# A pad of 96 bytes in front of nine weight buffers, and nine different starts inside them

## The chip, the cores and the metric

The kernel runs on one core of one Trainium2 chip. The metric is device time in microseconds (us) of one execution, the median of several. A profile of one execution stands beside it; its engines are called PE (TensorE, matmuls), PEld (TensorE's weight loads), DVE (VectorE), ACT (ScalarE), POOL (GpSimd) and SP (the queue that issues nearly all transfers).

## What is computed

A trunk of two layers over 256 tokens of width 2048, in float32. Each layer is an attention (two kinds side by side in layer 0, a differential one in layer 1), a cross-attention to 256 memory tokens and an MLP, each between two norms:

```
h = h + rms_norm(attention(rms_norm(h)) @ w_out)
h = h + rms_norm(memory_cross_attention(rms_norm(h), mem_n, wq, wk, wv, wo))
u = relu(rms_norm(h) @ w_up)          # 2048 -> 8192
h = h + rms_norm((u * u) @ w_down)    # 8192 -> 2048
```

Nearly all of the time is spent in products of 256 tokens with weights that are read once.

## The kernel before

**Three matmuls for a product.** Every float32 operand is kept as two parts, a rounded one and the rest (`[:, 0]` and `[:, 1]` of a tile). `mm3` (L252) makes a product of three matmuls: high by high, high by low, low by high. A matmul has a *stationary* operand (128 x 128, brought in by a weight load) and a *moving* one (up to 512 columns that stream through). Each of the matmuls here has a weight load of its own, which runs on PEld while the matmul before it streams.

**Weights.** `Weights.load` (L174) brings 256 rows x 512 columns (512 KB) into `raw`; ACT writes the rounded part into a tile `w` (L185 or, with a gain, L190), DVE the rest (L186, L191). `w` comes from the pool `wp` with `NW = 9` buffers in rotation, called homes here. At most nine are alive (`live`), so ACT's next split waits until PE has used up a home. Eleven of the `w` tiles in the whole program lie elsewhere ("spare", in tiles of attention that are free at the time).

**Three shapes of work on PE.** `in_step` (L259): stationary a slice of `xT` (the activations), moving a row of 512 columns of `w`; 6 matmuls for a home and a token tile. `out_block` (L287): stationary a slice of `lt`, moving `w`; a chunk is 12 matmuls, 6 from one home and 6 from the next, then the same two homes for the other token tile. `up` (L683), for 15 of 16 groups of each layer's MLP: the other way round, stationary a slice of `w`, moving `xT`; for each of 64 places in a block a matmul of 512 columns (L715) and one of 256 (L716). An `up` block is followed by an `out_block` of 96 matmuls that uses the `ut` of the group before.

**Behind an `up` block** its four sums lie in three PSUM banks `at` and in one of the three banks `mm`. `split_u` (L671) takes them in two pairs: ACT copies one half of a bank to `ue` (L676), DVE adds the other half to it (L677), then ACT does relu and square (L678, L679) and both engines split the result. The next `out_block` takes the other two `mm` banks for its first two chunks and this one for its third.

**Order.** PE's instructions stand in the order in which the code issues them (a `Line` of delayed calls mixes the attention pieces in). The order on ACT and DVE is made by the scheduler from what each buffer allows.

**Where things lie.** The pools lay tiles one behind the other in each partition's memory. In the built program `xT` begins at byte 33,920, the first home at 71,200 and the others every 8,192 bytes, `lt` at 207,904 (or at 187,424 where `qT`'s buffer is used), `qT` at 187,424, `kT` at 169,504, `v` at 177,696. Every slice that a matmul reads begins at a multiple of 512 bytes inside its tile. So a home's rows begin a multiple of 512 bytes from those of `lt`, and 96 bytes short of a multiple of 512 from those of `xT`. `kT`, `qT` and `v` are whole multiples of 512 from one another too.

Of the kernel before, what the change touches and what calls it, by code (L numbers as in the profile page):

```python
# [11 lines left out]
F32 = mybir.dt.float32  # L12
F32R = mybir.dt.float32r
# [5 lines left out]
P = 128  # L19
D = 2048  # L20
S = 256
# [7 lines left out]
NA_KW = 16  # L29
NW = 9  # L30
NPB = 2
NG = 16
D_TR, D_EV, D_ROPE = 8, 3, 8
SW_GAP, SW_T, SW_M = 4, 8, 7
# [36 lines left out]
def trunk(  # L71
# [6 lines left out]
    V, A, G, PE = nc.vector, nc.scalar, nc.gpsimd, nc.tensor  # L78

    keep = ctx.enter_context(tc.tile_pool(name="keep", bufs=1))  # L80
    wp = ctx.enter_context(tc.tile_pool(name="wp", bufs=NW))
    rawp = ctx.enter_context(tc.tile_pool(name="rawp", bufs=3))
    gp = ctx.enter_context(tc.tile_pool(name="gp", bufs=1))
    sb = ctx.enter_context(tc.tile_pool(name="sb", bufs=1))
# [35 lines left out]
    class Line:  # L120
        def __init__(self):
            self.now, self.q, self.n = 0, [], 0
# [29 lines left out]
    class Weights:  # L152
        def __init__(self):
            self.specs, self.tiles, self.n, self.wait, self.open = [], {}, 0, [], set()
            self.goal, self.live = -1, 0

        def plan_in(self, src, n0, g, spare=(), gate=None):

# [7 lines left out]
        def plan_out(self, src, k0):  # L166
# [4 lines left out]
                    self.specs.append((src, k0 + 2 * kp, n * 512, None, None, None))  # L171
            return a

        def load(self, j):  # L174
            src, k0, n0, tag, _, g = self.specs[j]
            raw = rawp.tile([P, 2, 512], F32, tag="raw", name="raw")
            nc.sync.dma_start(
                raw, src[k0 * P : (k0 + 2) * P, n0 : n0 + 512].rearrange("(k p) n -> p k n", p=P)
            )
            if tag is None:  # L180
                w = wp.tile([P, 2, 2, 512], F32R, tag="w", name="w")
            else:
                w = sb.tile([P, 2, 2, 512], F32R, tag=tag, bufs=1, name="w")
            if g is None:
                A.copy(w[:, 0], raw)  # L185
                V.tensor_tensor(w[:, 1], raw, w[:, 0].bitcast(F32), ALU.subtract)  # L186
            else:
                for kk in range(2):
                    gk = gains[:, g * KT + k0 + kk : g * KT + k0 + kk + 1]
                    A.activation(w[:, 0, kk], raw[:, kk], AF.Copy, scale=gk)  # L190
                    V.scalar_tensor_tensor(  # L191
                        w[:, 1, kk], raw[:, kk], gk, w[:, 0, kk].bitcast(F32), ALU.mult, ALU.subtract
                    )
            self.tiles[j] = w
# [74 lines left out]
    def in_block(u, evac, lag=0, between=None):  # L269

        pts = {}
        for i in range(8 + lag):
            for t, kp in enumerate((i, i - lag)):
                if not 0 <= kp < 8:
                    continue
                if kp == 0:
                    pts[t] = mm_ps()
                in_step(pts[t], u, kp, t)
                if kp == 7 and lag:
                    evac(t, pts[t])  # L280
                    if between is not None:
                        between(t)
        if not lag:
            for t in range(NT):
                evac(t, pts[t])
# [69 lines left out]
    class Leave:  # L355
# [10 lines left out]
        def __call__(self, t, n, c):  # L366
# [3 lines left out]
            if n == 3 and c.space != bass.MemoryType.PSUM:  # L370
                ys[3] = sb.tile([P, 512], F32, tag="p", bufs=NPB, name="y3")
            V.tensor_tensor(ys[n], c, self.post[:, n * 512 : (n + 1) * 512], ALU.mult)
# [76 lines left out]
    def qT_tile():  # L449
        return sb.tile([P, 2, NT, 4, P], F32R, tag="qT", bufs=1, name="qT")  # L450
# [16 lines left out]
    def softmax(sc, bias=None, snk=None):  # L467

        p = sb.tile([P, NT, S], F32, tag="p", bufs=NPB, name="p")
        m = sm.tile([P, NT], F32, tag="m", name="m")  # L470
# [117 lines left out]
    def plan_rest(l, o):  # L588
# [5 lines left out]
        U["up", l, 0] = W.plan_in(mlp_w_up[l], 0, G_MLP + l, ("qT", "kT", "v"), ("up", l))  # L594
        for g in range(NG):
            if g + 1 < NG:
                U["up", l, g + 1] = W.plan_in(mlp_w_up[l], 512 * (g + 1), G_MLP + l)
# [38 lines left out]
    def mem_x(t, n):  # L636
        d = sb.tile([P, 4, P], F32, tag="mt", bufs=2, name="mt")
        nc.sync.dma_start(d, memT[:, t, 4 * n : 4 * n + 4, :])
        split_x(t, n, d)
        I.x[t, n] = "mem"  # L640
# [10 lines left out]
    def mem_and_mlp(l, R, kT, nxt):  # L651
        qT = qT_tile()

        def between(t):
            for n in range(4):
                mem_x(t, n)

        in_block(U["mq", l], evac_T(qT, R, q=True, ev=D_EVM), lag=L_MQ, between=between)
        v = v_tile()
        hd = Heads(qT, kT, lambda i: i, v, lambda i: i, tags=("pT", "pT", "qT", "kT"), lag=(ME_GAP, ME_T, ME_M)).start(M_AT, mix=False)  # L660
        in_block(U["mv", l], evac_V(v, RSM), lag=L_MV)
        for i in range(4):
            line.until(lambda: hd.pT[i] is not None)
            hd.mix(i)
        lv = Leave(gain(mem_post_g[l : l + 1]), G_MLP + l)
        hd.finish()
        W.free(("up", l))
        out_block(U["mo", l], hd.lt, True, lv, stagger=True)
        R = lv.next

        def split_u(ut, j, pts):  # L671

            s = sb.tile([P, 512], F32, tag="p", bufs=NPB, name="s")
            for i, pt in enumerate(pts):
                e = sb.tile([P, S], F32, tag="ue", bufs=2, name="ue")
                A.copy(e, pt[:, S:])  # L676
                V.tensor_tensor(s[:, i * S : (i + 1) * S], pt[:, :S], e, ALU.add)  # L677
            A.activation(s, s, AF.Relu)  # L678
            A.activation(s, s, AF.Square)  # L679
            d = [ut[:, a, j : j + 2, :].rearrange("p k c -> p (k c)") for a in range(2)]  # L680
            split_to(d[0], d[1], s)

        def up(g):  # L683
            ut = lt_tile(("lt", "qT")[g % 2])
            if g == 0:
                left = [0, 1]

                def ev(t, pt):
                    q = sb.tile([P, 512], F32, tag="q", bufs=2, name="u")
                    A.activation(q, pt, AF.Relu)  # L690

                    def turn():
                        tp = tr_ps()
                        for i in range(4):
                            PE.transpose(tp[:, i * P : (i + 1) * P], q[:, i * P : (i + 1) * P], ident)
                        s = sb.tile([P, 512], F32, tag="p", bufs=NPB, name="s")
                        A.activation(s, tp, AF.Square)
                        sv = s.rearrange("p (k c) -> p k c", c=P)
                        split_to(ut[:, 0, :, t * P : (t + 1) * P], ut[:, 1, :, t * P : (t + 1) * P], sv)

                    line.later(D_EVU, turn)

                in_block(U["up", l, 0], ev, lag=L_UP)
                return ut
            pts = [at_ps() for _ in range(3)] + [mm_ps()]
            for kp in range(8):
                w = W.get(U["up", l, g] + kp)
                for t in range(NT):
                    line.until(lambda: I.has_x(t, kp // 2, False))
                for nt in range(4):  # L710
                    for kk in range(2):
                        kt = 2 * kp + kk
                        wn = [w[:, a, kk, nt * P : (nt + 1) * P] for a in range(2)]
                        both = xT[:, kt].rearrange("p a t c -> p (a t c)")
                        PE.matmul(pts[nt], wn[0], both, start=kt == 0, stop=False)  # L715
                        PE.matmul(pts[nt][:, :S], wn[1], both[:, :S], start=False, stop=kt == KT - 1)  # L716
                    if nt == 3:
                        W.done(U["up", l, g] + kp)
                    line.tick()
            for b in range(2):  # L720
                split_u(ut, 2 * b, pts[2 * b : 2 * b + 2])
            return ut

        uts = {0: up(0)}
        lv = None
        for g in range(NG):
            if g + 1 < NG:
                uts[g + 1] = up(g + 1)
            last = g == NG - 1
            if last and l == 0:  # L730
                W.free("odd")
            if last:
                eps = []
                for r in R:
                    q = sm.tile([P, 1], F32, tag="r2", name="r2")
                    V.tensor_tensor(q, r, r, ALU.mult)
                    V.reciprocal(q, q)
                    V.tensor_scalar(q, q, q, NEPS, ALU.mult, ALU.mult)
                    eps.append(q)
                lv = Leave(gain(mlp_post_g[l : l + 1]), nxt, eps)  # L740
            out_block(U["dn", l, g], uts.pop(g), g == 0, lv, stagger=last)
        return lv.next
# [41 lines left out]
    for c in START[2]:  # L784
        t = int(c.lower() == "b")
# [190 lines left out]
```

## Time and profile before

| | us |
|---|---|
| median of 3 runs | 2392.57 (2389.25 to 2392.69) |
| the profiled execution's own time | 2397.27 |
| its span, first to last instruction | 2395.4 |
| PE busy | 2368.5 (99%) |
| DVE busy | 1611.1 (67%) |
| ACT busy | 1373.6 (57%) |

The own time is 1.87 us more than the span. A row of the timeline that ends in xN stands for N instructions of one kind in a row; its second number runs from the start of the first to the end of the last. A matmul's own duration (some 390 ns at 512 columns) is longer than its distance to the next one, since they are pipelined: the distance is (length of the row - duration of one) / (N - 1).

### The profile page before, as it was taken

How to read it: one execution, taken by the hardware profiler on the slowest of the kernel's cores; microseconds unless marked ns; L12 is line 12 of the kernel's file. 1: busy time of each engine (PE TensorE's matmuls, PEld its weight loads, DVE VectorE, ACT ScalarE, POOL GpSimd, SP SyncE). 2: the span in 40 equal slices, each digit the busy share in tenths (PEclk: the TensorE clock that was granted, in tenths of full speed). 3: DMA queues.
4: the chain of work that ended last, by engine and by line, in shares of the span. 5: the costliest groups of instructions: out<-in, count | busy, mean ns of one | idle time of the engine just before them, and what ended most of it. 6: DMA issues, size and time to landing. Idle time of an engine off the chain costs nothing.

```text
span 2395.4 us, 32033 instructions
## 1 busy us (share of the span) xinstructions
PE 2368.5 (99%) x11687; PEld 1984.7 (83%) x11687; DVE 1611.1 (67%) x2545; ACT 1373.6 (57%) x2280; POOL 27.6 (1%) x46
## 2 busy tenths in 40 slices
PE   8999999999999999999999999999999999999998
PEld 6788887888888888888888888887888888888887
DVE  5775678856666656656875666787665666666666
ACT  6756567765555545545665645676754555555553
POOL 0000000000000000000000000000000000000000
PEclk9999999999999999999999999999999999999999
DMA  7657665565665666665555555555656566666663
GB/s 240 214 173 236 185 200 181 180 201 186 192 195 183 194 194 181 196 195 186 184 188 169 168 183 170 197 176 174 201 193 193 184 197 191 187 194 185 192 195 114
DMA packets 238278, 451.88 MB, mean 189 GB/s; under 512 B 21288, under 2 KB 22184, under 8 KB 237352
## 3 DMA queue, kind: packets, MB, share of 16 engines
q1 hardware_dynamic: 237832, 449.32, 59.1%
q8 instruction: 91, 1.49, 0.3%
q14 instruction: 67, 0.55, 0.1%
q10 hardware_dynamic: 288, 0.52, 0.1%
HBM read 445.59 MB, written 5.15 MB: 188 GB/s over the span
## 4 chain that ended last, share of the span: by engine, by line
PE 92%; DMA 3%; DVE 3%; ACT 1%; issue 1%; POOL 0%; SPq 0%; DVEq 0%; POOLq 0%; ACTq 0%
PE mm L254 60%; PE at L715 14%; PE at L716 7%; PE mm L715 5%; PE mm L716 2%; PE at L254 2%; DVE w L191 1%; DMA raw<-in_even_w_in 1%; DMA raw<-in_mem_wv 1%; DMA raw<-in_mem_wo 1%; DMA mt<-memT 1%; PE tr L432 1%; PE tr L345 1%; PE at L502 1%; DMA h<-in_x 0%
## 5 line engine op out<-in xcount | busy, mean ns | idle before, releaser
L254 PE MATMUL mm<-w,lt 128*128 128x512 f32 x4032 | 928.1, 390 | 0.0
L254 PEld LDWEIGHTS mm<-w,lt 128*128 128x128 f32 x4032 | 752.6, 188 | 156.3 <-DVE lt L396 0.3
L191 DVE SCALAR_TENSOR_TENSOR w<-raw,gains,w 128x512 fp32r<-128x512 f32 x944 | 678.1, 746 | 271.4 <-ACT w L190 269.8
L190 ACT ACTIVATE w<-raw,gains 128x512 fp32r<-128x512 f32 x944 | 636.1, 717 | 362.6 <-PE mm L254 269.4
L254 PE MATMUL mm<-w,xT 128*128 128x512 f32 x2784 | 689.6, 401 | 1.2 <-ACT q L424 0.8
L186 DVE TENSOR_TENSOR w<-raw,w 128x1024 fp32r<-128x1024 f32 x336 | 411.1, 1224 | 386.6 <-ACT w L185 386.1
L254 PEld LDWEIGHTS mm<-w,xT 128*128 128x128 f32 x2784 | 515.9, 190 | 115.7 <-ACT q L424 1.2
L185 ACT CAST w<-raw 128x1024 fp32r<-128x1024 f32 x336 | 352.1, 1048 | 448.9 <-PE mm L716 337.2
L715 PE MATMUL at<-xT,w 128*128 128x512 f32 x1440 | 514.8, 393 | 0.0
L716 PE MATMUL at<-xT,w 128*128 128x256 f32 x1440 | 401.8, 279 | 0.0
L715 PEld LDWEIGHTS at<-xT,w 128*128 128x128 f32 x1440 | 269.8, 187 | 64.2
L716 PEld LDWEIGHTS at<-xT,w 128*128 128x128 f32 x1440 | 270.0, 187 | 1.2
L309 DVE TENSOR_TENSOR y<-mm,y 128x512 f32<-128x512 f32 x256 | 175.3, 685 | 16.1 <-PE mm L254 15.9
L715 PE MATMUL mm<-xT,w 128*128 128x512 f32 x480 | 178.3, 393 | 0.0
L716 PE MATMUL mm<-xT,w 128*128 128x256 f32 x480 | 133.9, 279 | 0.0
L715 PEld LDWEIGHTS mm<-xT,w 128*128 128x128 f32 x480 | 89.9, 187 | 21.5
L716 PEld LDWEIGHTS mm<-xT,w 128*128 128x128 f32 x480 | 89.9, 187 | 0.0
L676 ACT COPY ue<-at 128x256 f32<-128x256 f32 x90 | 33.4, 371 | 31.1 <-PE mm L715 28.6
L396 DVE TENSOR_TENSOR lt<-s,lt 128x512 fp32r<-128x512 f32 x64 | 44.0, 688 | 3.6 <-ACT lt L395 3.6
L254 PEld LDWEIGHTS at<-kT,qT 128*128 128x128 f32 x240 | 35.7, 196 | 11.8 <-ACT qT L395 5.3
L254 PE MATMUL at<-kT,qT 128*128 128x256 f32 x240 | 38.5, 294 | 6.8 <-ACT qT L395 4.4
L318 ACT ACTIVATE junk<-y 128x512 bf16<-128x512 f32 x32 | 20.1, 629 | 38.9 <-DVE y L304 38.8
(113 smaller groups left out, 1063.0 us busy)
## 6 DMA issues: line engine op xcount, KB each, us to landing
raw<-in_mlp_w_up SPq DMA_DIRECT2D x256, 512.0 KB, 3.8
raw<-in_mlp_w_down SPq DMA_DIRECT2D x256, 512.0 KB, 4.2
raw<-in_odd_w_in SPq DMA_DIRECT2D x96, 512.0 KB, 4.3
raw<-in_even_w_in SPq DMA_DIRECT2D x72, 512.0 KB, 4.6
raw<-in_even_w_out SPq DMA_DIRECT2D x32, 512.0 KB, 4.4
raw<-in_odd_w_out SPq DMA_DIRECT2D x32, 512.0 KB, 3.8
mt<-memT SPq DMA_DIRECT2D x32, 256.0 KB, 4.2
raw<-in_mem_wk SPq DMA_DIRECT2D x16, 512.0 KB, 4.2
```

What stands on the lines that cost most here:

```text
L185: A.copy(w[:, 0], raw)
L186: V.tensor_tensor(w[:, 1], raw, w[:, 0].bitcast(F32), ALU.subtract)
L190: A.activation(w[:, 0, kk], raw[:, kk], AF.Copy, scale=gk)
L191: V.scalar_tensor_tensor(w[:, 1, kk], raw[:, kk], gk, w[:, 0, kk].bitcast(F32), ALU.mult, ALU.subtract)
L254: PE.matmul(pt, lhs(a), rhs(b), start=first and i == 0, stop=last and i == 2)
L309: V.tensor_tensor(ysl, pt, ysl, ALU.add)
L345: PE.transpose(pt[:, i * P : (i + 1) * P], h[:, t, k * P : (k + 1) * P], ident)
L396: V.tensor_tensor(lo, src, hi.bitcast(F32), ALU.subtract)
L432: PE.transpose(tp[:, i * P : (i + 1) * P], u[:, i * P : (i + 1) * P], ident)
L676: A.copy(e, pt[:, S:])
L715: PE.matmul(pts[nt], wn[0], both, start=kt == 0, stop=False)
L716: PE.matmul(pts[nt][:, :S], wn[1], both[:, :S], start=False, stop=kt == KT - 1)
```

## The change

A tile of 24 float32 numbers (96 bytes) is put in front of the pool `wp`. The rotation of nine buffers becomes nine tiles `wa` to `wi` of one buffer each, taken in turn, each 64 numbers (256 bytes) longer than a home needs; a home begins `HOMES[i]` numbers into its tile, that is 0, 4, 8, 12, 16, 24, 240, 248 and 48 bytes. `ue` has one buffer in place of two.

```diff
+X_SHIFT = 24
+HOMES = (0, 1, 2, 3, 4, 6, 60, 62, 12)
...
-    wp = ctx.enter_context(tc.tile_pool(name="wp", bufs=NW))
+    shift = ctx.enter_context(tc.tile_pool(name="shift", bufs=1))
+    shift.tile([P, X_SHIFT], F32, name="shift")
+    wp = ctx.enter_context(tc.tile_pool(name="wp", bufs=1))
...
-            self.goal, self.live = -1, 0
+            self.goal, self.live, self.turn = -1, 0, -1
...
+        def home(self):
+
+            i = self.turn = (self.turn + 1) % NW
+            c, e = "abcdefghi"[i], HOMES[i]
+            t = wp.tile([P, 2 * 2 * 512 + 64], F32R, tag=f"w{c}", name=f"w{c}")
+            return t[:, e : e + 2 * 2 * 512].rearrange("p (a k n) -> p a k n", a=2, k=2)
...
-                w = wp.tile([P, 2, 2, 512], F32R, tag="w", name="w")
+                w = self.home()
...
-                e = sb.tile([P, S], F32, tag="ue", bufs=2, name="ue")
+                e = sb.tile([P, S], F32, tag="ue", bufs=1, name="ue")
```

In the built program the tiles `wa` to `wi` now begin at 71,296 and every 8,448 bytes (33 x 256), and what lies behind them moves too: `lt` to 210,304 (or 189,824), `qT` to 189,824, `kT` to 171,904, `v` to 180,096. `xT` stays. Taken modulo 256, `xT`, `lt`, `qT`, `kT`, `v` and the tiles `wa` to `wi` all begin at 128, so that a home's distance from both `xT` and `lt` is its own offset (modulo 512 every second home is 256 away from `xT`, and the others from `lt`).

PE's and SP's instructions stand in the same order as before. On ACT and DVE the order changes behind each `up` block. ACT's rows of one block, before (`ue<-at` and `ue<-mm` are the copies of `split_u`, `s<-s` relu and square, `lt<-s` the split's first half, `w<-raw` the splits of weights):

```order
L676 COPY ue<-at 128x256 x3
L190 ACTIVATE w<-raw,gains 128x512
L678 ACTIVATE s<-s 128x512
L676 COPY ue<-mm 128x256
L679 ACTIVATE s<-s 128x512
L190 ACTIVATE w<-raw,gains 128x512
L395 CAST lt<-s 128x512
```

and of the change (its lines are 11 further down):

```order
L687 COPY ue<-at 128x256 x2
L201 ACTIVATE we<-raw,gains 128x512
L689 ACTIVATE s<-s 128x512
L687 COPY ue<-at 128x256
L690 ACTIVATE s<-s 128x512
L201 ACTIVATE we<-raw,gains 128x512
L406 CAST lt<-s 128x512
L687 COPY ue<-mm 128x256
```

The copy from the bank `mm` moves from the fourth copy in a row of six instructions to a place behind the first pair's relu, square and split. DVE's rows of the same block, before (`s<-mm` is the addition that is the last to read the bank `mm`, `y<-mm` takes the sum of a chunk of the next `out_block`):

```order
L677 TENSOR_TENSOR s<-at,ue 128x256 x3
L191 SCALAR_TENSOR_TENSOR w<-raw,gains,w 128x512
L677 TENSOR_TENSOR s<-mm,ue 128x256
L309 TENSOR_TENSOR y<-mm,y 128x512
L396 TENSOR_TENSOR lt<-s,lt 128x512
```

and of the change:

```order
L688 TENSOR_TENSOR s<-at,ue 128x256 x2
L202 SCALAR_TENSOR_TENSOR we<-raw,gains,we 128x512
L688 TENSOR_TENSOR s<-at,ue 128x256
L320 TENSOR_TENSOR y<-mm,y 128x512
L407 TENSOR_TENSOR lt<-s,lt 128x512
L688 TENSOR_TENSOR s<-mm,ue 128x256
```

The last read of the bank `mm` moves behind the first chunk's `y<-mm` and the first pair's `lt<-s`.

## Rows read from the trace of the kernel before

**Rows 1.** The page: span, busy time by engine, granted clock of TensorE by slices.

```profile
span 2395.4 us, 32033 instructions
...
PE 2368.5 (99%) x11687; PEld 1984.7 (83%) x11687; DVE 1611.1 (67%) x2545; ACT 1373.6 (57%) x2280; POOL 27.6 (1%) x46
...
PEclk9999999999999999999999999999999999999999
```

**Rows 2.** Groups by line and shape, PE: busy us, mean ns, idle before.

```profile
L254 PE MATMUL mm<-w,lt 128*128 128x512 f32 x4032 | 928.1, 390 | 0.0
...
L254 PE MATMUL mm<-w,xT 128*128 128x512 f32 x2784 | 689.6, 401 | 1.2 <-ACT q L424 0.8 <-DVE v L400 0.5
...
L715 PE MATMUL at<-xT,w 128*128 128x512 f32 x1440 | 514.8, 393 | 0.0
...
L715 PE MATMUL mm<-xT,w 128*128 128x512 f32 x480 | 178.3, 393 | 0.0
```

**Rows 3.** Waits, longest first: who waited for whom, us in total, times, longest.

```profile
ACT w L185 <- PE mm L716: 337.2, 194, 1.8
...
ACT w L190 <- PE mm L254: 269.4, 160, 3.2
...
PE at L572 <- DMA graw<-in_mem_norm_g: 6.0, 1, 6.0
PE at L254 <- ACT qT L395: 4.4, 3, 2.1
```

**Rows 4.** Timeline of PE: an up block and the out_block behind it.

```profile
1013.60 0.40 PE L715 MATMUL at<-xT,w 128*128 128x512 f32 x1
...
1035.89 0.28 PE L716 MATMUL mm<-xT,w 128*128 128x256 f32 x1
1036.01 21.96 PE L254 MATMUL mm<-w,lt 128*128 128x512 f32 x96
```

**Rows 5.** Timeline of PE: a long row of in_steps, and attention matmuls of 256 columns.

```profile
1329.76 14.21 PE L254 MATMUL mm<-w,xT 128*128 128x512 f32 x60
1343.81 0.87 PE L254 MATMUL at<-kT,qT 128*128 128x256 f32 x6
```

**Rows 6.** Timeline of PE in narrow windows behind a change of form.

```profile
1036.01 2.01 PE L254 MATMUL mm<-w,lt 128*128 128x512 f32 x8
...
1037.40 2.21 PE L254 MATMUL mm<-w,lt 128*128 128x512 f32 x9
...
1294.40 2.00 PE L254 MATMUL mm<-w,lt 128*128 128x512 f32 x8
...
1317.11 2.03 PE L254 MATMUL mm<-w,xT 128*128 128x512 f32 x8
```

**Rows 7.** Timeline of ACT and DVE behind the same up block.

```profile
1034.36 0.82 ACT L676 COPY ue<-at 128x256 f32<-128x256 f32 x2
1036.14 0.37 ACT L676 COPY ue<-at 128x256 f32<-128x256 f32 x1 [0.95 <-PE mm L715]
1036.41 0.73 ACT L190 ACTIVATE w<-raw,gains 128x512 fp32r<-128x512 f32 x1
1037.03 0.62 ACT L678 ACTIVATE s<-s 128x512 f32<-128x512 f32 x1
...
1037.81 0.64 ACT L679 ACTIVATE s<-s 128x512 f32<-128x512 f32 x1
...
1038.95 0.61 ACT L395 CAST lt<-s 128x512 fp32r<-128x512 f32 x1
...
1035.63 0.75 DVE L677 TENSOR_TENSOR s<-at,ue 128x256 f32<-128x256 f32 x2
...
1037.95 0.42 DVE L677 TENSOR_TENSOR s<-mm,ue 128x256 f32<-128x256 f32 x1
1038.97 0.69 DVE L309 TENSOR_TENSOR y<-mm,y 128x512 f32<-128x512 f32 x1 [0.60 <-PE mm L254]
1039.60 0.69 DVE L396 TENSOR_TENSOR lt<-s,lt 128x512 fp32r<-128x512 f32 x1
```

## The prediction

> **What bounds the kernel.** I read the page first. PE is busy for 2368.5 of 2395.4 us, and TensorE's clock is granted in full (the 2.4 GHz level) in every slice [rows 1]. ACT and DVE have room, and what ACT mostly waits for is PE, to give a home free: 337.2 and 269.4 us [rows 3]. PE's own waits are short; the two longest sums are 6.0 and 4.4 us [rows 3]. So the time is the number of matmuls times the distance from one to the next, and only a change of these distances, or a new wait of PE, moves the end.
>
> Next I worked out the distances, since a busy PE need not be PE at its best. In an `out_block` 96 matmuls take 21.96 us: (21.96 - 0.39) / 95 = 227.1 ns each [rows 4]. In a row of `in_step`s 60 take 14.21 us: (14.21 - 0.40) / 59 = 234.1 ns [rows 5]. Both stream the same 512 columns from the same homes in the same order high, low, high; only the stationary operand differs. The mean durations tell the same, 390 against 401 ns [rows 2]. An `up` block's 64 pairs take 1036.01 - 1013.60 = 22.41 us, 350.2 ns a pair [rows 4]; a 256-column matmul costs (0.87 - 0.28) / 5 = 118 ns [rows 5], which leaves 232 ns for the 512-column one. The groups show no idle time before these matmuls [rows 2].
>
> What goes with this difference is the place in memory. Where it is 227.1 ns, stationary and moving slices begin a multiple of 512 bytes apart; where it is 232 to 234 ns, they are 96 bytes off (32 modulo 64). The weight load for the next matmul reads memory while the present one streams, so I take it that the two reads get in each other's way by an amount that hangs on their distance.
>
> A third thing matters here: the 227.1 ns is reached only after some matmuls. Behind an `up` block the first eight of the `out_block` are (2.01 - 0.39) / 7 = 231.4 ns apart, the next nine (2.21 - 0.39) / 8 = 227.5 [rows 6]; behind `in_step`s the first eight are 230.0 apart [rows 6]; the other way round, the first eight `in_step`s are 232.9 [rows 6]. It looks like a rhythm that has to settle.
>
> **The pad and the homes.** The pad brings the tiles `wa` to `wi` to the same place modulo 256 as `xT`, and everything behind them to that place too. With no offsets every pair of slices would have distance 0 (modulo 256). The offsets then give nine distances, modulo 64: 0, 4, 8, 12, 16, 24, -16, -8, -16. None of these is in the trace; they lie between the two that are, 0 (227.1) and 32 (234.1), and those are the bounds for each home.
>
> *Lower bound:* all homes as at distance 0. The 4032 `out_block` matmuls stay; 2784 `in_step` ones gain 7.0 ns, 19.5 us; 1920 pairs go from 350.2 to 227.1 + 118 = 345.1, 9.8 us. Sum: -29.3 us.
>
> *Upper bound:* only `wa`, with offset 0, does well, the other eight cost 234.1, or 350.2 a pair. `out_block`: 4032 x 8/9 x 7.0 = +25.1 us. `in_step`: of the 2784, 11 spare tiles x 12 = 132 gain in any case (0.9 us), and a ninth of the other 2652 gains 2.1 us. Pairs: a ninth of 9.8, 1.1 us. Sum: +21.0 us.
>
> *What I take.* Four homes (0, 4, 8, -8) are much nearer to 0 than to 32; I give them the settled 227.5 of [rows 6]. The other five lie near the middle, and a home lasts only 6 matmuls in an `out_block` before one with another offset follows, fewer than the eight that [rows 6] shows unsettled; I give them 231.4. The mean is (4 x 227.5 + 5 x 231.4) / 9 = 229.7 ns. `out_block`: 2.6 x 4032 = +10.5 us. `in_step`: -4.4 x 2652 - 0.9 = -12.6 us. Pairs: 229.7 + 118 = 347.7 against 350.2, -2.5 x 1920 = -4.8 us. Sum: -6.9 us. The sign turns where the mean over the homes is (4032 x 227.1 + 2652 x 234.1 + 1920 x 232.2) / 8604 = 230.4 ns, close above what I take, so the sign is far from safe.
>
> **One `ue` buffer.** ACT's second copy must now wait for DVE's first addition, and the bank `mm` is read last, behind the first pair's work. By the durations in [rows 7]: DVE's first addition still starts at 1035.63, the second copy at about 1036.05, then a split (0.73), relu (0.62), the third copy (0.37), square (0.64), a split (0.73) and a cast (0.61), each started some 0.1 us before the end of the one ahead (1037.03 against 1036.41 + 0.73): the copy from `mm` starts near 1039.5. On DVE `y<-mm` ends at 1039.66 as now, `lt<-s` follows to 1040.3 and the last addition (0.42) to about 1040.7. PE's third chunk wants the bank at 1036.01 + 24 x 0.227 = 1041.46, its weight load 0.23 earlier. So about half a microsecond of cover is left, and I cost it at nothing. Without the cover each 0.5 us would come 30 times, 15 us. `ut` is wanted a whole `up` block later, and the weight splits that stand behind these in ACT's queue have the waits of [rows 3] as slack.
>
> **Writing to odd places.** ACT and DVE write to starts that are no multiple of 16 bytes. If they got slower by a tenth they would still be below PE (DVE 1611 us, ACT 1374 [rows 1]); nothing. Transfers go to `raw` as before, on the same queue in the same order.
>
> **Sum.** -6.9 us on the span of 2395.4 makes 2388.5. The profiled execution's own time, 2397.27, is 4.7 us above the median of the runs; I take the difference off the median: 2392.57 - 6.9 = 2385.7, rounded to 2386.
>
> **Rivals.**
>
> *All homes settle* (the lower bound): 2392.6 - 29.3 = 2363. For it: [rows 6] shows a rhythm that, once caught, holds over 80 matmuls, and an offset of some bytes may not break it. Against it: 12 to 24 bytes is half way to the distance that does break it.
>
> *Only equal starts settle* (the other side). With 231.4 for the eight other homes the same sums give +15.4 - 9.1 - 2.7 = +3.6 us, with 234.1 they give +21.0; in the middle 2405. For it: homes change every 6 matmuls, so no rhythm has time to form; and if the pattern repeats over 512 bytes, every second home is 256 off against `xT` and the rest against `lt`. Against it: `xT` is now near for all homes. It decides from a mean of 230.4 ns over the homes on.
>
> *Addresses do not matter.* Then 227 against 234 ns has another cause, such as the order of tiles, nothing moves, and the time is 2392.6. The Trainium skill says this, in "TensorE: Matmul & The Clock Gate", Part 2: TensorE has two independent read ports, and loading the next weights takes no read bandwidth from the running matmul. By it the sum would be 0. For it: ACT's and DVE's reads and writes beside PE leave no mark that I could find. Against it: the same moving rows at two distances, in [rows 4, 5].
>
> *The third chunk waits* behind the bank `mm`: with 0.5 us a block, 2385.7 + 15 = 2401. Against it: the half microsecond of cover.
>
> **Chances and range.** The forecast's own case 0.35 (2377 to 2393); all settle 0.2; only equal starts 0.25; addresses do not matter 0.15; the third chunk 0.05. A measurement of this kernel tells a change from none at about 0.2%, 4.8 us. Faster than that: all of the second case and seven tenths of the first, 0.45. Within it: most of "do not matter" and some of the first, 0.22. Slower: 0.33. The range leaves out the outer half of "all settle" and the worst of "only equal starts": 2362 to 2412.
>
> **What would show it.** The tiles are now named `wa` to `wi`, so the groups of matmuls by tile should show nine durations: near 390 ns for `wa`, `wb`, `wc`, `wh`, and nearer 394 to 397 for the rest, much alike whether `xT` or `lt` is stationary. In an `up` block a pair should depend on its home. An `out_block` behind an `up` block should take (95 x 229.7 + 390) ns, 22.2 us, in place of 21.96, a long row of `in_step`s less than 234 each. An idle time of PE before the third chunk would show the `ue` buffer. I am wrong if the offsets act otherwise than by nearness to 0: if the 4-byte start is among the worst, or if the sides against `lt` and `xT` differ.

## The result and the profile after

The changed kernel takes 2406.03 us (median of 3 runs, 2401.05 to 2406.9) against 2392.57: a ratio of 1.0057, 95% interval 1.004 to 1.0075. It is slower by 0.57%, 13.5 us. The forecast was 2386, faster; the measured time lies inside its range and on the other side of no change.

The page of the profiled execution (own time 2406.03 us; its lines answer to [rows 1]):

```profile
span 2404.3 us, 32057 instructions
...
PE 2380.4 (99%) x11687; PEld 1988.3 (83%) x11687; DVE 1613.0 (67%) x2545; ACT 1371.3 (57%) x2280; POOL 28.0 (1%) x46
...
PEclk9999999999999999999999999999999999999999
```

As before PE is busy for 99% of the span, with the same number of matmuls; the mean granted clock is 0.998, before it was 0.997. Of PE's waits the longest answers to that of [rows 3]:

```profile
PE at L583 <- DMA graw<-in_mem_norm_g: 5.7, 1, 5.7
```

No new wait came in, and none before the third chunk. So each matmul has become longer in distance to the next ("spacing" from here on, to keep it apart from the distance of two addresses). Where, the chain of work in order of time shows. Its columns are the start, the time from this start to that of what follows, engine, line and count. Of the kernel before, the first and last `out_block`s of the two MLPs:

```profile
505.72 21.77 PE mm L254 x96
...
1080.38 21.80 PE mm L254 x96
...
1724.43 21.77 PE mm L254 x96
...
2299.09 21.80 PE mm L254 x96
```

The same places after, with layer 0's third and fourth `out_block` too:

```profile
505.14 22.27 PE mm L265 x96
...
594.22 22.26 PE mm L265 x96
638.76 22.28 PE mm L265 x96
...
1084.50 22.28 PE mm L265 x96
...
1727.31 22.28 PE mm L265 x96
...
2306.66 22.26 PE mm L265 x96
```

By stages the whole difference of the spans is there: up to the first of these rows -0.6 us, layer 0's MLP 579.36 against 574.66 us, +4.7, from there to layer 1's MLP 642.81 against 644.05, -1.2, layer 1's MLP +4.7, the rest of the span +1.3. Together +8.9, which is 2404.3 - 2395.4. Only the two +4.7 are firm. The profiled execution of the kernel before was 4.7 us above its median, and the run "Everything moved by 96 bytes" below, which has all its spacings, takes the same 574.66 us in layer 0's MLP but 502.18 us up to its first `out_block` and 641.51 us between the MLPs, 3.5 and 2.5 less; against it these two stages of the change are 3.0 and 1.3 us longer. Its rows:

```profile
502.18 21.77 PE mm L257 x96
...
1076.84 21.80 PE mm L257 x96
...
1718.35 21.77 PE mm L257 x96
```

By forms of work: an `out_block` matmul has gone from 21.80 / 96 = 227.1 ns to 22.26 / 96 = 231.9. A pair in an `up` block has gone from 350.2 ns [rows 4] to (638.76 - 594.22 - 22.26) / 64 = 348.1. For `in_step` the timeline of PE, in a long row that mixes the two kinds, shows every home by itself:

```profile
1322.04 3.01 PE L265 MATMUL mm<-wb,xT 128*128 128x512 f32 x12
1324.89 2.97 PE L265 MATMUL mm<-wc,xT 128*128 128x512 f32 x12
1327.69 2.92 PE L265 MATMUL mm<-wd,xT 128*128 128x512 f32 x12
1330.45 2.93 PE L265 MATMUL mm<-we,xT 128*128 128x512 f32 x12
1333.22 2.96 PE L265 MATMUL mm<-wf,xT 128*128 128x512 f32 x12
1336.02 2.99 PE L265 MATMUL mm<-wg,xT 128*128 128x512 f32 x12
1338.85 2.96 PE L265 MATMUL mm<-wh,xT 128*128 128x512 f32 x12
1341.65 2.94 PE L265 MATMUL mm<-wi,xT 128*128 128x512 f32 x12
1344.44 2.89 PE L265 MATMUL mm<-wa,xT 128*128 128x512 f32 x12
1347.17 1.59 PE L265 MATMUL mm<-wb,xT 128*128 128x512 f32 x6
```

From one start to the next, over 12, the spacing of each home is: `wb` (4 bytes) 2.85 / 12 = 237.5 ns, `wc` (8) 233.3, `wd` (12) 230.0, `we` (16) 230.8, `wf` (24) 233.3, `wg` (240) 235.8, `wh` (248) 233.3, `wi` (48) 232.5 and `wa` (0) 227.5. The mean, (1347.17 - 1322.04) / 108, is 232.7 ns. The start of a home alone makes a difference of 10 ns, and the worst start is the one that lies nearest to the best.

The sum by these spacings: `out_block` 4.8 ns x 4032 = +19.3 us, `in_step` (232.7 - 234.1) x 2784 = -3.9, pairs -2.1 x 1920 = -4.0. Together +11.4 us, between the difference of the two spans (+8.9) and that of the medians (+13.5).

### The profile page after: what moved, and what is told of

Same layout as the page of the kernel before. It is cut to its first block, busy times and chain, and to the rows that moved or that the text cites. A ratio compares the mean times of both kernels' runs of the same rounds, so it can differ in the third digit from the quotient of the medians.

```text
span 2404.3 us, 32057 instructions
## 1 busy us (share of the span) xinstructions
PE 2380.4 (99%) x11687; PEld 1988.3 (83%) x11687; DVE 1613.0 (67%) x2545; ACT 1371.3 (57%) x2280; POOL 28.0 (1%) x46
## 4 chain that ended last, share of the span: by engine, by line
PE 92%; DMA 3%; DVE 2%; ACT 2%; issue 1%; SPq 0%; POOL 0%; DVEq 0%; POOLq 0%; ACTq 0%
PE mm L265 60%; PE at L726 14%; PE at L727 7%; PE mm L726 5%; PE mm L727 2%; PE at L265 2%; DMA raw<-in_mem_wv 1%; DMA raw<-in_even_w_in 1%; DMA raw<-in_mem_wo 1%; DMA mt<-memT 1%; ACT junk L329 1%; PE tr L443 1%; PE tr L356 1%; PE at L513 1%; DMA h<-in_x 0%
## 5 line engine op out<-in xcount | busy, mean ns | idle before, releaser
L265 PE MATMUL mm<-wh,lt 128*128 128x512 f32 x468 | 121.9, 395 | 0.0
L265 PE MATMUL mm<-wa,lt 128*128 128x512 f32 x468 | 120.4, 392 | 0.0
L265 PE MATMUL mm<-wc,lt 128*128 128x512 f32 x456 | 118.3, 394 | 0.0
L265 PE MATMUL mm<-wf,lt 128*128 128x512 f32 x444 | 116.6, 397 | 0.0
L265 PE MATMUL mm<-we,lt 128*128 128x512 f32 x444 | 115.1, 394 | 0.0
L265 PE MATMUL mm<-wg,lt 128*128 128x512 f32 x444 | 114.8, 394 | 0.0
L265 PE MATMUL mm<-wb,lt 128*128 128x512 f32 x432 | 114.0, 399 | 0.0
L265 PE MATMUL mm<-wd,lt 128*128 128x512 f32 x444 | 113.8, 391 | 0.0
L265 PE MATMUL mm<-wi,lt 128*128 128x512 f32 x432 | 112.1, 394 | 0.0
L265 PEld LDWEIGHTS mm<-wh,lt 128*128 128x128 f32 x468 | 87.7, 189 | 19.6
L265 PEld LDWEIGHTS mm<-wa,lt 128*128 128x128 f32 x468 | 87.4, 188 | 19.5
L265 PEld LDWEIGHTS mm<-wb,lt 128*128 128x128 f32 x432 | 81.3, 189 | 19.3
```

The lines of the kernel that those rows point to most:

```text
L265: PE.matmul(pt, lhs(a), rhs(b), start=first and i == 0, stop=last and i == 2)
```

## The experiments

Each run is compared with runs of the kernel before on the same chip: 2393.32 us for the first four, 2391.71 for the next four, 2388.51 (a single run) for the last three.

**The pad alone.** Homes as before, one behind the other; everything lies at the same place modulo 256.

```diff
+X_SHIFT = 24
+    shift = ctx.enter_context(tc.tile_pool(name="shift", bufs=1))
+    shift.tile([P, X_SHIFT], F32, name="shift")
```

> The pad of 96 bytes alone: homes in rotation every 8,192 bytes as before, all at distance 0 from xT and lt. Theory D (the distance between the starts of stationary and moving slices sets the spacing, and the nine unlike starts spoil what the pad gives): out_block stays at 227 ns, in_step falls from 234 to about 227, an up pair from 350 to about 345, so some 29 us less than before, near 2363. Theory N (addresses play no part; the loss came from the one ue buffer): no change, within 5 us of before.

2388.2 us, ratio 0.998 (0.9971 to 0.999). The groups by line and shape, which answer to the second and the third of [rows 2]:

```profile
L257 PE MATMUL mm<-w,xT 128*128 128x512 f32 x2784 | 675.3, 396 | 1.9 <-ACT q L427 1.5 <-DVE v L403 0.4
...
L718 PE MATMUL at<-xT,w 128*128 128x512 f32 x1440 | 519.3, 398 | 0.0
```

`in_step` loses 14.3 us of its busy time (689.6 before), 5.1 ns a matmul, and the `up` block gets longer: its 512-column matmul goes from 393 to 398 ns. The chain gives a pair, and the long row:

```profile
497.83 21.79 PE mm L257 x96
542.22 21.79 PE mm L257 x96
...
1293.95 41.53 PE mm L257 x183
```

(542.22 - 497.83 - 21.79) / 64 = 353.1 ns, where before it was 350.2. The long row holds 69 `out_block` matmuls and 114 `in_step` ones: (41.53 - 69 x 0.2270) / 114 = 226.9 ns for an `in_step`, 234.1 before [rows 5]. So distance 0 is good for the two forms in which the weights move and bad for the one in which they are stationary. 2.9 x 1920 = +5.6 us eats a good part of the gain: -14.3 + 5.6 = -8.7 us by rows, 5.1 measured.

**All homes at 4 bytes.** The change with one start for all.

```diff
-HOMES = (0, 1, 2, 3, 4, 6, 60, 62, 12)
+HOMES = (1, 1, 1, 1, 1, 1, 1, 1, 1)
```

> The change with all nine homes 4 bytes into their tiles. Theory M (a single start, whatever it is within some bytes, lets the rhythm settle; the loss came from the change of start every 6 matmuls): spacing near 227 in out_block and in_step, some 25 to 29 us less than before. Theory O (each offset has its own spacing, alone or mixed): home wb's 237 ns in out_block and 238 in in_step everywhere, so about 40 + 8 us more than before, near 2440. Theory N: as the change, about 2405.

2435.95 us, ratio 1.0179 (1.0162 to 1.0196), close to Theory O's 2440 and outside the prediction's range. The chain:

```profile
1049.75 22.78 PE mm L265 x96
1094.93 22.78 PE mm L265 x96
...
1320.22 43.40 PE mm L265 x183
```

An `out_block` matmul takes 237.3 ns with no change of start from home to home; of the last row, (43.40 - 69 x 0.2373) / 114 = 237.1 ns fall on an `in_step` matmul. A pair, (1094.93 - 1049.75 - 22.78) / 64 = 350.0, is where it was. So it isn't the mixture of starts that costs, as the rival "only equal starts settle" had it: the offset itself does, and 4 bytes cost more than the 32 of before.

**One `ue` buffer alone**, in the kernel before.

```diff
-                e = sb.tile([P, S], F32, tag="ue", bufs=2, name="ue")
+                e = sb.tile([P, S], F32, tag="ue", bufs=1, name="ue")
```

> Before with one ue buffer in place of two, nothing else. Theories D, M and O: the cover of about half a microsecond holds, no change (within 3 us). Theory N: the loss of the change, 13 us, is here.

2392.2 us, ratio 0.9998 (0.9988 to 1.0007). No cost can be seen.

**A scan in one run.** Every group of the MLPs has its own start, for its `up` and its `out_block` homes; everything else starts at 0.

```diff
+SCAN = ((0, 1, 2, 3, 4, 5, 6, 7, 8, 10, 12, 14, 16, 24, 32, 48), (0, 63, 62, 61, 60, 58, 56, 52, 40, 36, 9, 11, 13, 15, 20, 17))
...
-            c, e = "abcdefghi"[i], HOMES[i]
+            c, e = "abcdefghi"[i], self.off.get(j // 8, 0)
...
+            W.off[U["up", l, g] // 8] = W.off[U["dn", l, g] // 8] = SCAN[l][g]
```

> The change with one start for all homes of an up group and of the out_block that uses it, another for each of the 32 groups: 0 to 48 bytes in steps of 4 or 8 and up to 252 in layer 1; 0 elsewhere. A map of spacing by offset with no mixing inside a block of 96 or 128 matmuls. Theory M: the small offsets (up to 8 or 16 bytes either way) settle at 227 behind the first matmuls of a block, those near 32 stand at 231 to 235. Theory O: 4 bytes at 237, 12 bytes at 229, 24 at 235 as in the nine homes. In both 64 and 128 bytes tell over how many bytes the pattern repeats: at 227 if over 64.

2399.4 us in one run; the time says little, the chain all. In layer 0 these are the `out_block`s at 0, 4, 8, 12 and 16 bytes, one block for each start, and the last row is the one at 240 bytes in layer 1:

```profile
498.76 21.79 PE mm L265 x96
542.75 22.79 PE mm L265 x96
587.94 22.40 PE mm L265 x96
632.56 21.97 PE mm L265 x96
677.14 22.23 PE mm L265 x96
...
1896.03 21.76 PE mm L265 x96
```

The second column over 96 is the spacing of an `out_block`; what lies between a row's end and the next start, over 64, is a pair of the `up` block for the group after the next (between the first two rows the one at 8 bytes: (542.75 - 498.76 - 21.79) / 64 = 346.9). Read in this way, from these rows and from the others of the same chain (ns; a part of the starts; the pairs at 4 and 252 are from the timeline of each layer's first `up` block, without the break for four transposes):

| bytes past distance 0 | `out_block` | pair in `up` |
|---|---|---|
| 0 | 227.0 | 353.1 (the pad alone) |
| 4 | 237.4 | 350.0 |
| 8 | 233.3 | 346.9 |
| 12 | 228.9 | 350.0 |
| 16 | 231.6 | 347.2 |
| 20 | 236.6 | 353.3 |
| 24 | 233.3 | 346.9 |
| 28 | 227.8 | 353.1 |
| 32 | 233.2 | 353.1 |
| 48 | 233.2 | 346.9 |
| 64 | 229.1 | 353.1 |
| 160 (`xT` before) | 234.4 | 350.0 |
| 240 | 226.7 | 353.1 |
| 244 | 239.4 | 346.9 |
| 248 | 232.6 | 351.6 |
| 252 | 229.0 | 348.8 |

The map isn't a slope from 0 to 32. It goes up and down within 8 bytes, 64 is not as good as 0, and the two forms want different starts. One order does show over the 28 `out_block`s of the chain, by the start modulo 16: those at 12 are all good (12, 28, 44, 60, 252: 227.8 to 230.0 ns), those at 4 hold the worst (4, 20, 36, 52, 244: 233.6 to 239.4), those at 8 lie between (8, 24, 40, 56, 232, 248: 232.5 to 233.8). The multiples of 16 have no such order (226.7 at 240, 234.6 at 208), nor have the pairs. The map gives back what was known: the 234 and 350 ns of before at 160, which is the distance of its homes from `xT`.

**A start for each use.** 0 for homes that move, 24 bytes for those that are stationary in `up`.

```diff
-HOMES = (0, 1, 2, 3, 4, 6, 60, 62, 12)
+H_IO, H_UP = 0, 6
...
-            c, e = "abcdefghi"[i], HOMES[i]
+            c, e = "abcdefghi"[i], H_UP if j // 8 in self.ups else H_IO
...
+                W.ups.add(U["up", l, g + 1] // 8)
```

> The change with the start chosen by the use of the home and not by its letter: 0 where it is the moving operand (out_block, in_step), 24 bytes where it is the stationary one (up groups 1 to 15). Theory O (each distance has its own spacing, a different one for each form, whatever stood in the home before): out_block 227.5, in_step 228.5, a pair 346.7 as in the scan, against 227.7, 234.4 and 350.2 before: some 16 + 7 = 23 us less, near 2370. Theory M (unlike starts in turn spoil the rhythm): a loss at every change between an up group and an out_block, so no better than the pad alone, 2388.

2375.84 us, ratio 0.9933 (0.9918 to 0.9948): better than both kernels, though 15.9 us below the kernel before where Theory O had 23. The chain:

```profile
501.21 21.77 PE mm L265 x96
...
1028.73 21.77 PE mm L265 x96
1072.69 21.77 PE mm L265 x96
1291.37 41.53 PE mm L265 x183
...
1708.35 21.77 PE mm L265 x96
```

A pair takes (1072.69 - 1028.73 - 21.77) / 64 = 346.7 ns; in the long row an `in_step` matmul takes (41.53 - 69 x 0.2268) / 114 = 227.0 ns, 234 before. Layer 0's MLP takes 1072.69 - 501.21 = 571.48 us, 3.2 less than before. From its last `out_block` to layer 1's first there are 635.66 us, 5.9 less than the 641.51 of the run with everything moved and 8.4 less than the 644.05 of the execution profiled before the change.

**240 bytes in place of 0** (226.7 in the scan), 24 for `up`.

```diff
-H_IO, H_UP = 0, 6
+H_IO, H_UP = 60, 6
```

> As e5_by_form with 240 bytes in place of 0 for the moving homes. The scan had one block at 240 bytes, at 226.7 ns. Theory O: out_block 226.7, and in_step alike, another 3 to 5 us less than e5_by_form. If a block's spacing hangs on chance besides its distance (one block is one sample), out_block comes out higher.

2418.38 us, ratio 1.0115 (1.0098 to 1.0132). The scan's value did not come back; the chain has, in every block,

```profile
548.93 22.71 PE mm L265 x96
```

22.71 / 96 = 236.6 ns. The same start at 226.7 in one run and 236.6 in another: the start of the moving homes alone doesn't set the spacing.

**0 and 240 in turn.** Neighbours in the rotation differ.

```diff
-HOMES = (0, 1, 2, 3, 4, 6, 60, 62, 12)
+HOMES = (0, 60, 0, 60, 0, 60, 0, 60, 0)
```

> The change with only two starts, 0 and 240 bytes, in turn from home to home. Each alone gave 227 ns in an out_block. Theory O: out_block stays at 227 to 228. Theory M: 230 or more, since the start changes every 6 matmuls. A pair of an up block 353 in both.

2393.57 us in one run. In the chain an `out_block` takes 22.07 us for its 96 matmuls. Out of one, three turns of six matmuls, with `we` at 0, `wf` at 240 and `we` again:

```profile
549.48 1.52 PE L265 MATMUL mm<-we,lt 128*128 128x512 f32 x6
550.84 1.56 PE L265 MATMUL mm<-wf,lt 128*128 128x512 f32 x6
552.24 1.52 PE L265 MATMUL mm<-we,lt 128*128 128x512 f32 x6
```

As a whole the block is at 22.07 / 96 = 229.9 ns, which is Theory M's figure and not the 227 to 228 of Theory O. But the loss isn't spread as M has it: the six matmuls from `we` take 1.36 / 6 = 226.7 ns each, those from `wf` 1.40 / 6 = 233.3. Homes at 0 keep their spacing, though a home at 240 comes after every six matmuls; this takes away the second leg of the rival "only equal starts settle". It is 240 bytes that has another spacing than the 226.7 of the scan.

**Everything moved by 96 bytes**, `xT` too: the pad stands ahead of the first pool, `keep`, in the kernel before.

```diff
+    shift = ctx.enter_context(tc.tile_pool(name="shift", bufs=1))
+    shift.tile([P, X_SHIFT], F32, name="shift")
     keep = ctx.enter_context(tc.tile_pool(name="keep", bufs=1))
```

> Before with the pad of 96 bytes in front of everything, xT too: every tile that matmuls read moves by 96 bytes and no distance changes. If the distance alone counts: spacings as before (227.1, 234.1, pair 350.2) and no change. If the place modulo 64 or 256 itself counts: out_block and in_step change places or both move, by 20 us or more either way.

2391.12 us, ratio 0.9997 (0.9988 to 1.0007), all spacings as before. At this step what counts is how the operands lie to one another, not where they lie. 96 is a multiple of 32, so the run says nothing of the place of odd starts (4 or 8 bytes).

**240 for moving homes and 232 for `up`**, as in the one block of the scan that had 226.7. Two explanations stood against each other by now: that a spacing belongs to the start alone, or that 240 has more than one rhythm, and what ran just before decides which is caught.

```diff
-H_IO, H_UP = 60, 6
+H_IO, H_UP = 60, 58
```

> As e6_240_24, with the up groups' homes at 232 bytes in place of 24. In the scan the out_block at 240 bytes, 226.7 ns, stood behind an up block at 232; in e6_240_24, behind up blocks at 24, all stood at 236.5. Theory R (at 240 bytes there is more than one rhythm, and what went before decides which is caught): out_blocks behind up blocks at 226.7 again, and about 10 ns x 2880 = 28 us less than e6_240_24. Theory C (the one block of the scan was another chance, such as a neighbour's start in the same homes): 236 as in e6_240_24.

2398.41 us in one run. The chain has an `out_block` behind an `up` block at

```profile
505.07 21.77 PE mm L265 x96
```

226.8 ns, and the timeline, for `out_block` matmuls in the attention, where no `up` block goes before,

```profile
249.85 1.58 PE L265 MATMUL mm<-wa,lt 128*128 128x512 f32 x6
...
255.52 1.58 PE L265 MATMUL mm<-wc,lt 128*128 128x512 f32 x6
```

(255.52 - 249.85) / 24 = 236.3 ns. Same start, same form, same execution: two spacings are there, and it goes with the `up` block ahead which one holds (24 bytes there: 236.6; 232 bytes: 226.8).

**`lt` alone moved**, by 252 bytes, in the kernel before. A home now begins 4 bytes past it (modulo 256), as in the run with all at 4 bytes, but it is the stationary side that has the odd start. The homes and `xT` stay.

```diff
+LT = 63
...
-        return sb.tile([P, 2, 4, S], F32R, tag=tag, bufs=1, name="lt")
+        t = sb.tile([P, 2 * 4 * S + 64], F32R, tag=tag, bufs=1, name="lt")
+        return t[:, LT : LT + 2 * 4 * S].rearrange("p (a k s) -> p a k s", a=2, k=4)
```

> Before, with lt 252 bytes into a tile 256 bytes longer, and nothing else moved but by multiples of 256: homes now begin 4 bytes past lt's place, modulo 256, without having moved themselves. Theory O in the form of a distance: out_block at 237 to 238 as with all homes at 4 bytes, in_step as before at 234, a pair as before at 350: some 40 us more. If it is the odd start of the moving operand that costs: out_block at 227 as before.

2414.43 us in one run. The groups by line and shape, and the chain:

```profile
L255 PE MATMUL mm<-w,lt 128*128 128x512 f32 x4032 | 952.7, 395 | 0.0
...
L255 PE MATMUL mm<-w,xT 128*128 128x512 f32 x2784 | 687.2, 400 | 1.5 <-ACT q L425 1.1 <-DVE v L401 0.4
```

```profile
1042.32 22.39 PE mm L255 x96
```

`out_block` goes from 227.1 to 233.2 ns, its busy time from 928.1 [rows 2] to 952.7 us, while `in_step`, which doesn't read `lt`, stays. The moving rows have not been touched, and the weight loads have not become longer (752.8 us in all and 188 ns on average, 752.6 and 188 before), so what a weight load reads beside a running matmul does cost that matmul time. But at the same 4 bytes the run with odd homes had 237.3, so the distance alone doesn't give the number.

**The nine starts in reverse order.**

```diff
-HOMES = (0, 1, 2, 3, 4, 6, 60, 62, 12)
+HOMES = (12, 62, 60, 6, 4, 3, 2, 1, 0)
```

> The change with its nine starts in reverse order (wa at 48 bytes, wb 248, wc 240 ... wi 0). Theory O pure: each start keeps the mean duration it had in the change (4 bytes 399 ns, 12 bytes 391, 0 bytes 392 in out_block), the total is the same. Theory R: some starts take other durations, since another start stands ahead of them; 240 bytes (394 in the change, 24 ahead of it) above all.

2404.15 us in one run, much as the change. By home, `wh` is now at 4 bytes and `wi` at 0 (mean durations, the second number behind the bar):

```profile
L265 PE MATMUL mm<-wh,lt 128*128 128x512 f32 x468 | 124.0, 400 | 0.0
L265 PE MATMUL mm<-wi,lt 128*128 128x512 f32 x432 | 111.2, 393 | 0.0
```

In the change the same view has for those at 0 and at 4 bytes:

```profile
L265 PE MATMUL mm<-wa,lt 128*128 128x512 f32 x468 | 120.4, 392 | 0.0
L265 PE MATMUL mm<-wb,lt 128*128 128x512 f32 x432 | 114.0, 399 | 0.0
```

So it is for all nine: each start has its mean of the change again, within 1 ns, in another home and behind another start. The start for which Theory R expected the most, 240 bytes, has 394 both times. In these mixtures the cost goes with the start, as Theory O has it.

## Why the prediction was wrong

**PE is full, and only spacings count:** right. PE's waits are those of before, and the MLPs, which repeat from run to run, are longer by what the spacings give.

**The place in memory makes the 227 and the 234 ns:** right, and now shown by the pad alone (`in_step` 234.1 to 226.9 in the long row), by all at 4 bytes and by `lt` alone. The rival "addresses do not matter" is gone. The rule of the Trainium skill that stood behind it ("TensorE: Matmul & The Clock Gate", Part 2: loading the next weights takes no read bandwidth from the running matmul) does not hold here in this form: with `lt` alone moved the running matmuls, their own data in place, went from 227.1 to 233.2 ns.

**What I take:** this is the step that failed: "Four homes (0, 4, 8, -8) are much nearer to 0 than to 32; I give them the settled 227.5". Nearness is not the measure. Of these four only 0 has 227.5; 4, 8 and -8 have 237.5, 233.3 and 233.3, while 12 and 16 bytes, put down as middling, have 230.0 and 230.8. In the long row the four near homes average 232.9 where 227.5 was put down, the other five 232.5 where 231.4 was. The mean over the homes was taken as 229.7 and is 232.7 in the long row of `in_step`s, 231.9 in the `out_block`s; the sign turned at 230.4. So `out_block` cost 19.3 us in place of 10.5, and `in_step` gave back 3.9 in place of 12.6; the pairs gave 4.0 of the 4.8. The prediction had named the 4-byte start among the worst as what would prove it wrong, and the group of `wb` was that.

**The bounds.** *Lower:* of its first two terms the pad alone has the first (`out_block` stays); the second, 19.5 us for `in_step`, measured 14.3, since the 7.0 ns of the long row were put on all 2784 matmuls and the mean gain is 5.1. The third, a pair at distance 0 as 227.1 + 118 = 345.1, was wrong: 353.1, worse than before. A spacing read in one form was carried to another. *Upper:* the sum held, but not its premise that nothing is worse than distance 32; 4 bytes are.

**One `ue` buffer and writes to odd places at nothing:** right (0.9998 for the one; ACT and DVE busy for 1371.3 and 1613.0 us, as before).

**The rivals.** "Only equal starts settle" gave 2405, the time that was measured, from a cause that the runs refute: equal starts at 4 bytes are the worst of all, and homes at 0 are fast between others. Half of its thought survives in another place, since at 240 bytes the spacing does hang on what else runs. That its figure agrees with the measurement is luck. Its doubt about 256 against 512 bytes has no support: `wb` is 256 off from `xT` modulo 512 and not from `lt`, `wa` the other way round, and with all moving homes at 0 ("A start for each use") every second one is 256 off on either side and both forms stay at 227 ns. "All settle" and "the third chunk waits" show in no row.

**What stays open.** Why a distance has its spacing, and why the order modulo 16 fails at the multiples of 16. What decides at 240 bytes: the `up` block ahead was changed together with the starts that ACT and DVE write to beside the `out_block`, and no run parts the two. Why 4 bytes cost 237 ns with the odd start on the moving side and 233 on the stationary one: another rhythm at the same distance, or a part that the start itself plays, are both possible, and no run tells them apart. And in the pad alone the sum by rows, 8.7 us, exceeds the measured gain of 5.1; a start for each use falls short of its sum in the same way, 15.9 of 23.

## What to carry over

Where PE is full and each matmul has a weight load of its own, read the spacing of every form of matmul from the timeline before anything else: the same 512 columns took from 227 to 239 ns here by how the stationary and the moving slice lie to each other, and the start for each use got 0.67% of the whole kernel. Don't fill in between two measured places; give each block of a repeated stage another start, and one run draws the map. Then measure the choice in the whole kernel, since a spacing seen in one block can belong to what ran ahead of it (240 bytes: 226.7 in the scan, 236.6 when all moving homes had it).

## What the runs showed of the hardware

- The spacing of matmuls of 512 columns, with a weight load each, goes up and down within a few bytes of the moving slice's start, counted from that of the stationary one: 227.0, 237.4, 233.3, 228.9, 231.6, 236.6, 233.3, 227.8 and 233.2 ns at 0, 4, 8, ... 32 bytes. Starts at 12 modulo 16 were good throughout (227.8 to 230.0); a multiple of 16 is no safe choice (226.7 to 234.6). The same 4 bytes made by moving the stationary operand gave 233.2.
- With the roles of the operands exchanged, and a matmul of 256 columns behind each of 512, the order is another one: 0 bytes are among the worst starts (353.1 ns a pair), 8, 16, 24 and 48 among the best (346.9 to 347.2).
- One distance can have several spacings: at 240 bytes 226.8 and 236.3 ns in one execution, behind an `up` block and away from one, and 233.3 where homes at 0 and at 240 take turns.
- Moving all tiles together by 96 bytes changes nothing that can be measured (0.9997).
